# A decoder kernel's gated part: two accumulators that shared a PSUM tile get tiles of their own, one pair's last products stand two slots earlier, and the norms' mean is made on ScalarE

## The chip, the cores and the metric

The kernel runs on one core of a Trainium2 chip. The metric is the time of one execution on the device in microseconds (us). A core has five engines with a queue of instructions each, which work at the same time and wait for each other by semaphores: TensorE (PE in the profile, with PEld for its weight loads), VectorE (DVE), ScalarE (ACT), GpSimd (POOL), and SyncE (SP), which issues the transfers between the chip's memory and the core. TensorE's results go to PSUM, which the other engines read.

## The reference

Two decoder layers work on 1024 tokens of width 1024. Each has a mixer (sparse attention in the first, forgetting attention in the second) beside a cross-attention into 256 memory tokens, one output projection, and a gated feed-forward part with a causal convolution of width three. What matters here is the last:

```python
def rms_norm(x, g):
    xf = x.astype(jnp.float32)
    y = xf * lax.rsqrt(jnp.mean(xf * xf, axis=-1, keepdims=True) + EPS)
    return (y * g.astype(jnp.float32)).astype(x.dtype)
# each layer ends with
x = x + jnp.concatenate([o_mix, o_mem], axis=-1) @ w_o[l]
x = x + conv_ffn(rms_norm(x, ffn_norm[l]), w_up[l], conv_w[l], conv_b[l], w_down[l])
# and conv_ffn, with D_FF = 2816:
#   u = h @ w_up            (1024 -> 2 x 2816)
#   u = causal depthwise convolution of u over the tokens, width 3, plus conv_b
#   a, b = the two halves of u
#   return (silu(a) * b) @ w_down
```

All data are float32.

## The kernel before, in words

**Products.** Every matrix product is made as three matmuls of float32r values: each operand is split into an upper part (made by ScalarE, `upper`, L86) and the rest, the lower part (made by VectorE, `lower`, L92), and `mm3` (L166 to L168) adds upper x upper, upper x lower and lower x upper into PSUM. In the names of tiles, `wh`, `vh` and `wl`, `vl` are upper and lower parts of weights; `hx` and `hT` hold both parts of the activations. A tile can be read or written by one engine only after the engine that used it before has signalled; such a dependence is kept for the tile as a whole.

**The gated part.** The up projection (class `Up`) works on 22 pairs of weight columns (128 of each of w_up's halves). For a pair the 2 x 2 block product with the activations is made in the seven products of the Strassen-Winograd scheme, each of twelve matmuls of 128 x 512. With p, q and c for the accumulators, in order:

1. first: a11 x b11 into p, copied to c1 by ScalarE;
2. second: a12 x b21 into q; c1 + q is one quarter of the result (L2001, or L2005 in the seam);
3. third: s2 x t2 is added into p, copied to c2;
4. fourth: s1 x t1 into c, copied to c5 (L1983);
5. t3: s3 x t3 is added into p; p + c5 is a quarter (L2036, VectorE);
6. b22: s4 x b22 is added into c; c + c2 is a quarter (L2039, VectorE);
7. t4: a22 x t4 is added into p; p is the last quarter (L2042, ScalarE).

The sums s1 to s4 of weights are made by GpSimd (L1458 to L1476 in the seam, L1942 to L1950 behind it), the sums t1 to t4 of activations by VectorE and GpSimd (L1430 to L1435). Then come the convolution (L2050 on ScalarE, L2052 on VectorE), the gate (L2059) and the stores.

**PSUM.** It is used as two tiles of two banks (`psa`) and four of one bank (`psb`); a bank holds 128 x 512 float32. Before, p and c of a pair are the two halves of one `psa` tile, and q is a `psb` tile (in the seam, q is written to c's half, since c comes later).

**Order behind the seam.** `Up.run` walks over slots; pair n's product i stands at slot 7n + 2i, so that two pairs are interleaved. TensorE's order is the written one for the first 17 slots, VectorE's and ScalarE's throughout the seam; elsewhere the instruction scheduler may still move rows. Pairs 0 and 1 start in the seam and have four of their products there.

**The seam.** Between the attention and the up projection, `gated` calls `seam` (L1296 on), which finishes the output projection, adds the residual (L1379), stores x (L1385), normalises each of the eight row tiles (square and sum on ScalarE L1390, mean and eps on VectorE L1396, power on GpSimd L1394, the scaling on VectorE L1398), transposes it on TensorE (`turn`, L1611) and starts pairs 0 and 1. Its order is made by a planner (`Order`): every step has an engine, a cost, a due time, the steps it comes after and the buffers it holds (`hold`), and the planner fixes the queues of TensorE, VectorE, ScalarE and GpSimd from these.

**The norms elsewhere** (`rstd`) take a square and sum on ScalarE (L127), the mean and eps on VectorE (L128), the power on GpSimd (L130), and the scaling on VectorE (L144 and others): at the start of the kernel for the eight tiles of x and two of memory, between the layers, and at the end.

## Time and profile before

| what | us |
|---|---|
| median of three runs | 2503.85 |
| lowest and highest run | 2503.02, 2506.69 |
| the profiled execution | 2505.03 |
| its span | 2503.0 |
| TensorE busy in the span | 2428.3 |
| VectorE busy | 1884.3 |
| ScalarE busy | 1351.8 |
| GpSimd busy | 737.0 |

The profile's rows are of one execution. A row has its start from the beginning of the span and its duration in us, the engine, the line of the kernel before, the operation with output and input, and in brackets the idle time of the engine before it with what ended it. TensorE's matmuls overlap: one of 128 x 512 shows about 0.39 us, and the next starts about 0.23 after it. The mean granted clock of TensorE was 0.995 of full speed. The first layer's seam lies around 640 to 740 us, the second's 1164.2 us later.

### The profile page before, as it was taken

What the parts mean: (1) busy time and instruction counts of PE and PEld (TensorE: products, weight loads), DVE (VectorE), ACT (ScalarE), POOL (GpSimd) and SP (SyncE); (2) the same over time, 40 slices, a digit from 0 to 9 for tenths busy, and PEclk for the clock granted to TensorE, in tenths of its full rate; (3) what the DMA queues carried; (4) which work ended last, traced back from release to release, by engine and by line L of the source; (5) the groups of instructions that cost most, each with busy time, mean ns of one, the idle gap of its engine ahead of it and who ended that gap; (6) DMA issues with size and microseconds to landing.
All of it is one profiled execution on the core that took longest, in us unless ns stands there. A gap on an engine that the chain in (4) does not pass through costs nothing.

```text
span 2503.0 us, 35524 instructions
## 1 busy us (share of the span) xinstructions
PE 2428.3 (97%) x12210; PEld 2040.0 (82%) x12210; DVE 1884.3 (75%) x3182; ACT 1351.8 (54%) x2583; POOL 737.0 (29%) x620
## 2 busy tenths in 40 slices
PE   7999999998989999999999999998999999999998
PEld 7788888877868888888889988887777888888886
DVE  5657999884597787879665478878578787788765
ACT  5335988884354454454455257757254454445444
POOL 0114455454165545430000000001235545551000
PEclk9999999999999999999999999999999999999999
DMA  8465233245423333367335567666613333339433
GB/s 251 134 211 165 69 86 101 81 141 165 163 64 114 99 103 109 98 228 247 93 126 174 159 179 204 184 177 192 218 68 106 101 102 110 96 101 318 164 95 121
DMA packets 303276, 357.68 MB, mean 143 GB/s; under 512 B 38024, under 2 KB 183288, under 8 KB 303096
## 3 DMA queue, kind: packets, MB, share of 16 engines
q1 hardware_dynamic: 303096, 355.41, 45.4%
q8 instruction: 97, 1.59, 0.3%
q14 instruction: 83, 0.68, 0.1%
HBM read 245.55 MB, written 109.78 MB: 142 GB/s over the span
## 4 chain that ended last, share of the span: by engine, by line
PE 80%; DVE 8%; DMA 4%; ACT 3%; issue 2%; POOL 1%; SPq 1%; POOLq 0%; DVEq 0%; ACTq 0%
PE psa L166 12%; PE psa L167 12%; PE psa L168 12%; PE psb L166 10%; PE psb L168 9%; PE psb L167 9%; PE psa L316 5%; PE psb L448 5%; PE psb L475 5%; DVE hT L92 1%; DVE wl L92 1%; DVE pt L462 1%; ACT ps L376 1%; DMA wr<-o 1%; ACT pt L459 1%
## 5 line engine op out<-in xcount | busy, mean ns | idle before, releaser
L2052 DVE SCALAR_TENSOR_TENSOR v<-u,cw,v 128x1023 f32<-128x1023 f32 (+1 forms) x176 | 276.7, 1572 | 67.7 <-ACT v L2050 66.1
L92 DVE TENSOR_TENSOR wl<-wr,wh 128x512 fp32r<-128x512 f32 (+2 forms) x244 | 229.2, 944 | 112.6 <-ACT wh L86 112.3
L86 ACT ACTIVATE wh<-wr 128x512 fp32r<-128x512 f32 (+2 forms) x244 | 182.3, 751 | 241.6 <-PE psa L168 109.8
L462 DVE TENSOR_TENSOR pt<-psb,pt 128x512 fp32r<-128x512 f32 (+2 forms) x380 | 247.0, 659 | 60.6 <-ACT pt L459 58.2
L2050 ACT ACTIVATE v<-u,cw 128x1024 f32<-128x1024 f32 x88 | 109.6, 1246 | 306.6 <-DVE u L2039 288.6
L459 ACT ACTIVATE pt<-psb 128x512 fp32r<-128x512 f32 (+2 forms) x380 | 215.6, 575 | 95.5 <-PE psb L448 92.3
L475 PE MATMUL psb<-pt,vv 128*128 128x512 f32 (+2 forms) x864 | 220.7, 355 | 5.2 <-DVE pt L462 4.1
L166 PE MATMUL psa<-hT,wh 128*128 128x512 f32 x560 | 218.4, 390 | 3.4 <-ACT hT L86 3.3
L167 PE MATMUL psa<-hT,wh 128*128 128x512 f32 x560 | 218.1, 389 | 1.5 <-DVE hT L92 1.5
L168 PE MATMUL psa<-hT,wl 128*128 128x512 f32 x560 | 217.9, 389 | 0.0
L316 PE MATMUL psa<-kk,qq 128*128 128x512 f32 (+4 forms) x792 | 177.3, 342 | 7.0 <-ACT pm L373 3.0
L376 ACT ACTIVATE ps<-ps,stat 128x640 f32<-128x640 f32 (+4 forms) x192 | 147.7, 773 | 28.7 <-DVE stat L356 28.5
L130 POOL TENSOR_TENSOR rs<-ss,consts 128x1 f32<-128x1 f32 x24 | 13.3, 555 | 492.0 <-DVE ss L128 320.0
L166 PE MATMUL psb<-hT,wh 128*128 128x512 f32 x384 | 156.0, 406 | 0.3 <-DVE pt L462 0.3
L475 PEld LDWEIGHTS psb<-pt,vv 128*128 128x128 f32 x864 | 136.5, 190 | 21.0 <-DVE pt L462 8.2
L448 PE MATMUL psb<-consts,ps 128*128 128x128 f32 x928 | 145.9, 274 | 6.6 <-DVE pt L462 1.7
L356 DVE CUSTOM_DVE_ANT_0 ps<-psa,caub 128x128 f32<-128x128 f32 (+1 forms) x192 | 139.6, 750 | 15.2 <-PE psa L316 13.4
L168 PE MATMUL psb<-hT,wl 128*128 128x512 f32 x384 | 151.0, 393 | 0.0
L167 PE MATMUL psb<-hT,wh 128*128 128x512 f32 x384 | 150.6, 392 | 0.0
L166 PE MATMUL psa<-hx,wh 128*128 128x512 f32 x352 | 137.9, 392 | 7.0 <-DVE u L2036 5.4
L316 PEld LDWEIGHTS psa<-kk,qq 128*128 128x128 f32 x792 | 122.5, 191 | 26.3 <-DVE stat L356 6.2
L539 POOL TENSOR_TENSOR wr<-wr 128x512 f32<-128x512 f32 x16 | 22.2, 1390 | 408.1 <-DMA kd<-st 241.3
(320 smaller groups left out, 6778.5 us busy)
## 6 DMA issues: line engine op xcount, KB each, us to landing
wr<-in_w_up_dram SPq DMA_DIRECT2D x88, 512.0 KB
wr<-gd SPq DMA_DIRECT2D x154, 256.0 KB
gd<-v SPq DMA_DIRECT2D x88, 256.0 KB
o<-ob SPq DMA_DIRECT2D x128, 128.0 KB
wr<-o SPq DMA_DIRECT2D x32, 512.0 KB
hT<-in_w_down_dram SPq DMA_DIRECT2D x64, 256.0 KB
gd<-gs SPq DMA_DIRECT2D x60, 256.0 KB
qd<-st SPq DMA_DIRECT2D x56, 256.0 KB
```

The lines of the kernel that those rows point to most:

```text
L86: self.nc.scalar.activation(hi, src, AF.Copy)
L92: self.nc.vector.tensor_tensor(lo, src, f32(hi), ALU.subtract)
L166: mm(out, lh, rh, start=first, stop=False, skip_group_check=more)
L167: mm(out, lh, rl, start=False, stop=False, skip_group_check=more)
L168: mm(out, ll, rh, start=False, stop=last, skip_group_check=more)
L316: nc.tensor.matmul(out, w, rhs, start=b not in banks[:i], stop=b not in banks[i + 1:])
L376: nc.scalar.activation(p, p, AF.Exp, bias=st[:, 0, ii:ii + 1], scale=-1.0, accum_out=st[:, 1, ii:ii + 1])
L448: nc.tensor.transpose(tp[0:kb, x:x + P], br["pt"][ii][:, o:o + kb], self.ident)
L459: nc.scalar.activation(st["hi"], st["src"], AF.Copy)
L462: self.nc.vector.tensor_tensor(st["lo"], st["src"], f32(st["hi"]), ALU.subtract)
L475: self.nc.tensor.matmul(out, v, t, start=st["begin"] and i == 0, stop=st["end"] and i == len(mms) - 1)
L2052: nc.vector.scalar_tensor_tensor(v[:, d:], u[:, :S - d], cw[:, tap, i:i + 1], v[:, d:], ALU.mult, ALU.add)
```

## The change

It has three parts.

- p becomes a `psb` tile of its own, and c the first half of a `psa` tile of its own, in the seam and behind it. In the seam the planner's holds follow, the second products no longer come after the copy of p, and the third products come after that copy rather than after the sum c1 + q.
- Pair 1's products t3, b22 and t4 stand at slots 13, 15 and 17 in place of 15, 17 and 19, and the copy of its fourth product is called at slot 11 in place of 10.
- The mean with eps is made by ScalarE, an Identity activation with a bias tile `eps`, in place of VectorE's tensor_scalar, in `rstd` and in the seam.

The numbers of lines in the changed kernel are four or five higher (L2036 becomes L2040, L2039 L2043, L2042 L2046, L1983 L1988, L166 L171, L1611 L1616, L1398 L1403, L1430 L1435, L1431 L1436).

```diff
+    def mean(self, ss):
+        self.nc.scalar.activation(ss[:, 1:2], ss[:, 0:1], AF.Identity, bias=self.eps, scale=1.0 / D)
+
     def rstd(self, pool, x, junk):
         nc = self.nc
         ss = self.sb(pool, [P, 2], F32, "ss", 4)
         nc.scalar.activation(junk, x, AF.Square, accum_out=ss[:, 0:1])
-        nc.vector.tensor_scalar(ss[:, 1:2], ss[:, 0:1], 1.0 / D, EPS, ALU.mult, ALU.add)
+        self.mean(ss)
...
-            q = o.add("ACT", 1.05, square, at + 2, a, [c])
-            m = o.add("DVE", 0.2, lambda: nc.vector.tensor_scalar(s["ss", t][:, 1:2], s["ss", t][:, 0:1], 1.0 / D, EPS, ALU.mult, ALU.add), at + 2.4, [q])
-            p = o.add("POOL", 0.52, power, at + 3, [m])
+            q = o.add("ACT", 1.25, square, at + 2, a, [c])
+            p = o.add("POOL", 0.52, power, at + 3, [q])
...
-        psas = [o.hold("psa", True) for _ in range(2)]
+        psas, psbs = [o.hold("psa", True) for _ in range(2)], []
         late = []
         for n in range(2):
             def go(n=n):
-                ac = self.psa()
-                st[n]["p"], st[n]["c"] = ac[:, :CH], ac[:, CH:]
+                st[n]["p"] = self.psb()
                 up.prod(n, st[n]["p"], "a11", "b11", True)
...
         turn(7)
         for n in range(2):
             def go(n=n):
-                st[n]["q"] = st[n]["c"]
+                st[n]["q"] = st[n]["c"] = self.psa()[:, :CH]
                 up.prod(n, st[n]["q"], "a12", "b21", True)
             hs = [psas[n]] + ([ha[1]] if n == 0 else [h1])
-            x = pe(4 * MM, go, [s["w", n, "a12" if n == 0 else "ra"], s["c1", n]] + parts["b21"], hs)
-            s["early", n] = o.add("DVE", 0.6, lambda n=n: up.take_early(n), now + 1.0, [x], [psas[n]])
+            x = pe(4 * MM, go, [s["w", n, "a12" if n == 0 else "ra"]] + parts["b21"], hs)
+            s["early", n] = o.add("DVE", 0.6, lambda n=n: up.take_early(n), now + 1.0, [x, s["c1", n]], [psas[n]])
...
-            x = s["third", n] = pe(4 * MM, lambda n=n: up.prod(n, st[n]["p"], "s2", "t2", False), [s["w", n, "21"], s["early", n]] + parts["t2"], [psas[n]])
+            x = s["third", n] = pe(4 * MM, lambda n=n: up.prod(n, st[n]["p"], "s2", "t2", False), [s["w", n, "21"], s["c1", n]] + parts["t2"], [psbs[n]])
...
     def first(self, n):
         s = self.st[n]
-        ac = self.k.psa()
-        s["p"], s["c"] = ac[:, :CH], ac[:, CH:]
+        s["p"], s["c"] = self.k.psb(), self.k.psa()[:, :CH]
...
-        at(10, self.copy_fourth, 1)
+        at(11, self.copy_fourth, 1)
...
-                    i, odd = divmod(slot - 7 * n, 2)
+                    i, odd = divmod(slot - 7 * n + (2 if n == 1 else 0), 2)
```

**How the order moves.** On TensorE, from pair 0's first product on, before the change (the first row of each group of twelve; `psa_7929` is pair 0's tile, `psa_7957` pair 1's, `psa_8222` pair 2's, `psb_8255` pair 2's q; the L1611 rows are the transposes of the last row tile). The rows are, from the top: pair 0's and pair 1's first products, pair 0's second, the transposes, pair 1's second, then further on pair 0's b22 and t4, pair 2's first, pair 1's t3, pair 2's second:

```order
L166 MATMUL psa_7929<-hx_7630,vh_7592 128x512
L166 MATMUL psa_7957<-hx_7630,wh_7881 128x512
L166 MATMUL psa_7929<-hx_7639,vh_7595 128x512
L1611 MATMUL psb_7999<-consts,x_7393 128x128 x4
L1611 MATMUL psb_8004<-consts,x_7393 128x128 x4
L166 MATMUL psa_7957<-hx_7639,wh_7881 128x512
...
L166 MATMUL psa_7929<-hx_7839,wh_8035 128x512
L166 MATMUL psa_7929<-hT_8072,vh_8078 128x512
L166 MATMUL psa_8222<-hx_7630,wh_8187 128x512
L166 MATMUL psa_7957<-hT_7995,wh_8164 128x512
L166 MATMUL psb_8255<-hx_7639,wh_8187 128x512
```

And with the change, the same groups (p of pairs 0, 1, 2 is `psb_7931`, `psb_7959`, `psb_8240`, c of pairs 0 and 1 `psa_7994` and `psa_8017`):

```order
L171 MATMUL psb_7931<-hx_7633,vh_7594 128x512
L171 MATMUL psb_7959<-hx_7633,wh_7885 128x512
L1616 MATMUL psb_7980<-consts,x_7395 128x128 x4
L1616 MATMUL psb_7987<-consts,x_7395 128x128 x4
L171 MATMUL psa_7994<-hx_7643,vh_7597 128x512
L171 MATMUL psa_8017<-hx_7643,wh_7885 128x512
...
L171 MATMUL psa_7994<-hx_7844,wh_8036 128x512
L171 MATMUL psb_7931<-hT_8076,vh_8079 128x512
L171 MATMUL psb_7959<-hT_8015,wh_8166 128x512
L171 MATMUL psb_8240<-hx_7633,wh_8191 128x512
```

The transposes of the last row tile moved ahead of both second products, and pair 1's t3 ahead of pair 2's first product; b22 now writes another tile than the t3 product before it.

On ScalarE, at the end of the seam, before (`c_8113` and `c_8160` are the copies of pair 0's and pair 1's fourth products, `wh_8164` the upper part of pair 1's s3 and s4, `hT_8072` the activations t4):

```order
L1983 ACTIVATE c_8093<-psa_7957 128x512
L86 ACTIVATE hT_8072<-x_7393 128x4x128 x2
L1983 ACTIVATE c_8113<-psa_7929 128x512
L1983 ACTIVATE c_8160<-psa_7957 128x512
L86 ACTIVATE wh_8164<-ws_8116 128x1024
L2050 ACTIVATE v_8181<-u_8141,cw_7357 128x1024
```

And with the change (`wh_8166`, `c_8115` and `c_8183` are the same three):

```order
L1988 ACTIVATE c_8096<-psb_7959 128x512
L86 ACTIVATE hT_8076<-x_7395 128x4x128 x2
L86 ACTIVATE wh_8166<-ws_8120 128x1024
L1988 ACTIVATE c_8115<-psa_7994 128x512
L86 ACTIVATE hT_8076<-x_7395 128x4x128
L1988 ACTIVATE c_8183<-psa_8017 128x512
L2054 ACTIVATE v_8185<-u_8145,cw_7359 128x1024
```

The split of pair 1's s3 and s4 moved ahead of both copies.

On VectorE, around the normalisation of the last row tile, before (L1398 is that normalisation, `psb_7923` and `psb_8004` the transposes of the last tile but one and of the last):

```order
L92 TENSOR_TENSOR hx_7839<-psb_7923,hx_7839 128x4x128
L1396 TENSOR_SCALAR ss_7945<-ss_7945 128x1
L92 TENSOR_TENSOR hT_7903<-x_7393,hT_7903 128x4x128
L92 TENSOR_TENSOR wl_7906<-ws_7501,wh_7905 128x1024
L1398 SCALAR_TENSOR_TENSOR x_7393<-x_7393,rs_7955,gb_7443 128x1024
```

And with the change:

```order
L92 TENSOR_TENSOR hT_7905<-x_7395,hT_7905 128x4x128
L92 TENSOR_TENSOR wl_7909<-ws_7503,wh_7908 128x1024
L1403 SCALAR_TENSOR_TENSOR x_7395<-x_7395,rs_7953,gb_7445 128x1024
L92 TENSOR_TENSOR hx_7844<-psb_7925,hx_7844 128x4x128
L92 TENSOR_TENSOR hT_7905<-x_7395,hT_7905 128x4x128
L1435 TENSOR_TENSOR x_7395<-psb_7980,x_7395 128x512
L1436 TENSOR_TENSOR x_7395<-psb_7987,x_7395 128x512
```

The mean is gone, and the eviction of the tile before (`hx`) moved behind the normalisation.

More of the change, by code (lines that the diff above doesn't have):

```diff
@@ L105, in constants @@
         self.nhalf = c[:, C_NH:C_NH + 1]
+        self.eps = cp.tile([P, 1], F32, name="eps")
+        nc.vector.memset(self.eps, EPS)
     def masks(self, pool, keep):
@@ L1390, in square @@
                 nc.scalar.activation(self.sb(up.pool, [P, CH], F32, "c", 5).bitcast(BF16), self.x[:, t, :], AF.Square, accum_out=s["ss", t][:, 0:1])
+                self.mean(s["ss", t])
             def power():
@@ L1552, in go @@
             def go(n=n):
-                ac = self.psa()
-                st[n]["p"], st[n]["c"] = ac[:, :CH], ac[:, CH:]
+                st[n]["p"] = self.psb()
                 up.prod(n, st[n]["p"], "a11", "b11", True)
-            hs = [psas[n]] + ([ha[0]] if n == 0 else [h1])
+            psbs.append(o.hold("psb", True))
+            hs = [psbs[n]] + ([ha[0]] if n == 0 else [h1])
             x = pe(4 * MM, go, [s["w", n, "a11" if n == 0 else "ra"]] + parts["b11"], hs)
@@ L1561, in copy @@
                 st[n]["c1"] = up.copied(st[n]["p"])
-            s["c1", n] = o.add("ACT", 0.48, copy, now + 0.8, [x], [c, psas[n]])
+            s["c1", n] = o.add("ACT", 0.48, copy, now + 0.8, [x], [c, psbs[n]])
         turn(7)
@@ L1580, in copy @@
                 st[n]["c2"] = up.copied(st[n]["p"])
-            o.add("ACT", 0.48, copy, now + 1, [x], [psas[n], c])
+            o.add("ACT", 0.48, copy, now + 1, [x], [psbs[n], c])
         for n in range(2):
```

## The prediction

> **What bounds the kernel now.** I read the busy shares first, then the busy time by stretch, then what TensorE waited for in the stretches that are not full, then the single rows there. The shares, from the head of the page:
>
> ```profile
> PE 2428.3 (97%) x12210; PEld 2040.0 (82%) x12210; DVE 1884.3 (75%) x3182; ACT 1351.8 (54%) x2583; POOL 737.0 (29%) x620
> ```
>
> TensorE sets the time nearly everywhere, so only its holes are worth anything. Busy time by stretch (length, then PE, PEld, DVE, ACT, POOL, granted clock, DMA share, GB/s), first layer's seam and what follows it:
>
> ```profile
> 700.00:710.00 10.00, 7.57 (x31) 5.44 (x30) 9.90 (x11) 6.97 (x13) 9.66 (x6) 1.00 0.00 0
> 710.00:720.00 10.00, 7.44 (x33) 5.82 (x31) 10.00 (x12) 1.61 (x4) 4.44 (x4) 1.00 0.20 57
> 720.00:730.00 10.00, 8.02 (x31) 5.68 (x32) 6.67 (x6) 7.49 (x9) 6.49 (x5) 1.00 0.36 101
> 800.00:1100.00 300.00, 300.00 (x1324) 248.08 (x1323) 236.56 (x190) 144.05 (x177) 152.30 (x91) 1.00 0.33 107
> ```
>
> TensorE has holes of about 7 us in 700 to 730, and none in 800 to 1100: what is won in the seam is kept, because behind it TensorE works without a break. VectorE is full from 700 to 720. What TensorE waited for between 690 and 800 (total, times, longest); three of its six lines; the second layer gives the same six:
>
> ```profile
> PE psa L166 <- DVE u L2036: 2.7, 1, 2.7
> ...
> PE psa L166 <- DVE u L2039: 0.8, 1, 0.8
> ...
> PE psa L166 <- ACT u L2042: 0.7, 1, 0.7
> ...
> ```
>
> And the rows themselves on TensorE (start, duration; in brackets the idle time before and its releaser):
>
> ```profile
> 694.05 0.39 PE L166 MATMUL psa<-hx,vh 128*128 128x512 f32 x1
> 696.80 1.04 PE L1611 MATMUL psb<-consts,x 128*128 128x128 f32 x8
> 702.21 0.47 PE L166 MATMUL psa<-hT,wh 128*128 128x512 f32 x1 [1.63 <-ACT hT L86]
> 703.43 0.50 PE L167 MATMUL psa<-hT,wh 128*128 128x512 f32 x1 [0.75 <-DVE hT L92]
> 720.15 0.50 PE L166 MATMUL psa<-hx,wh 128*128 128x512 f32 x1 [2.71 <-DVE u L2036]
> 723.97 0.51 PE L166 MATMUL psa<-hT,vh 128*128 128x512 f32 x1 [0.79 <-DVE u L2039]
> 727.74 0.50 PE L166 MATMUL psa<-hx,wh 128*128 128x512 f32 x1 [0.73 <-ACT u L2042]
> 728.80 0.50 PE L168 MATMUL psa<-hx,wl 128*128 128x512 f32 x1 [0.32 <-DVE wl L92]
> 733.91 0.39 PE L166 MATMUL psb<-hx,wh 128*128 128x512 f32 x1
> ```
>
> In order they are: pair 0's second product; the transposes of the last tile; pair 0's third product, with a hole at its start and one at its second matmul; pair 0's b22 product, its t4 product, pair 2's first product with two holes; and at 733.91 pair 2's second product, when pair 1's t3 product is done too. The waits behind b22 are of two kinds. The t4 product really needs L2036, because it adds into p, which L2036 reads. But b22 writes c, and L2036 reads p: it waits only because p and c are halves of one tile. The same holds for t4 waiting for L2039, which reads c, and for pair 2's first product, whose new tile is pair 0's whole old one.
>
> **The change, part by part.** *The waits across the halves* are 2.71 + 0.79 + 0.73 = 4.23 us a layer. Not all of it comes back, since VectorE is late itself:
>
> ```profile
> 693.47 1.49 DVE L1398 SCALAR_TENSOR_TENSOR x<-x,rs,gb 128x1024 f32<-128x1024 f32 x1 [0.74 <-DMA xm<-x]
> 701.98 0.68 DVE L92 TENSOR_TENSOR hx<-psb,hx 128x512 fp32r<-128x512 f32 x1
> 703.30 2.31 DVE L92 TENSOR_TENSOR wl<-ws,wh 128x1024 fp32r<-128x1024 f32 x1
> 711.84 1.21 DVE L92 TENSOR_TENSOR wl<-ws,wh 128x1024 fp32r<-128x1024 f32 x1
> 719.41 0.68 DVE L2036 TENSOR_TENSOR u<-psa,c 128x512 f32<-128x512 f32 x1
> 721.64 1.22 DVE L92 TENSOR_TENSOR wl<-ws,wh 128x1024 fp32r<-128x1024 f32 x1 [1.55 <-ACT wh L86]
> 723.22 0.69 DVE L2039 TENSOR_TENSOR u<-psa,c 128x512 f32<-128x512 f32 x1 [0.36 <-PE psa L168]
> 725.34 1.85 DVE L2052 SCALAR_TENSOR_TENSOR v<-u,cw,v 128x1023 f32<-128x1023 f32 x1 [1.43 <-ACT v L2050]
> 727.12 1.62 DVE L92 TENSOR_TENSOR wl<-wr,wh 128x1024 fp32r<-128x1024 f32 x1
> ```
>
> From 693.47 to the end of L2036 at 720.09 VectorE never waits. Its list up to there keeps its work, with one more row behind the last normalisation: an hx eviction that stood ahead of it (its like at 701.98 takes 0.68, some 0.6 in a row of them, since the next starts before it has ended). So L2036 of pair 0 ends at about 720.09 + 0.6 = 720.7, and t4 cannot start before.
>
> The b22 product, in between, now waits for ScalarE's copy of c alone. In ScalarE's new order a split stands ahead of that copy, whose input is GpSimd's second sum for pair 1, and GpSimd's first sum waits for the split's lower half at 711.84:
>
> ```profile
> 713.20 1.62 POOL L1473 TENSOR_TENSOR ws<-wr,wr 128x512 f32<-128x512 f32 x1 [3.03 <-DVE wl L92]
> 714.78 1.75 POOL L1476 TENSOR_TENSOR ws<-wr,ws 128x512 f32<-128x512 f32 x1
> 719.99 0.60 ACT L1983 ACTIVATE c<-psa 128x512 f32<-128x512 f32 x1 [7.30 <-POOL u L2010]
> 720.49 1.05 ACT L86 ACTIVATE wh<-ws 128x1024 fp32r<-128x1024 f32 x1
> 724.00 1.24 ACT L2050 ACTIVATE v<-u,cw 128x1024 f32<-128x1024 f32 x1 [2.46 <-issue]
> ```
>
> With the 0.6 above, GpSimd is done at 716.53 + 0.6 = 717.1, the split (1.05) at 718.2, the copy (0.60) at 718.8, b22 (a product is twelve matmuls, 694.05 to 696.80, 2.75) at 721.6. T4 starts there and not at 723.97: **2.4 us**.
>
> *Pair 1's last products two slots sooner* put its t3 between t4 and pair 2's first product. Its lower half is what VectorE now writes at 721.64, late by 1.55 through ScalarE, where pair 1's fourth copy stands ahead of the split and waits for a buffer (719.99 and 720.49 above). The change moves that copy behind, so the lower half follows L2036 at once, 720.7 to 721.9, and t3 runs from 724.3 to 727.0. Pair 2's first product comes then, no longer waiting for L2042. Its third matmul needs the lower half of 727.12: from 720.7 on VectorE has 1.2 (wl), 0.6 (L2039), 1.24 in which it waits for the convolution's first part on ScalarE (724.00), and 1.85 for the next (L2052), then this wl of 1.62, so 720.7 + 6.5 = 727.2, in time. Both are done at 729.8 instead of 733.91: 4.1 us. I take **3.6 a layer**, between 2.4 and 4.1 and nearer the upper, which counts further down the queue; the rest I leave because pair 3's lower half is then just in time on VectorE. Without pair 1's shift, pair 2's first product would follow t4 at 724.3 and stand until 727.2: the shift covers VectorE's lag.
>
> *The last transposes ahead of both second products.* TensorE reaches them at 694.05, not 696.80, and x's tile is done at 693.47 + 1.49 = 694.96, so TensorE waits 0.9 there, and everything behind in its queue with it, the two second products first. In return the halves of the last tile are made sooner, and the holes of 1.63 and 0.75 at 702.21 and 703.43 shrink by about 1.5. But the next product that needs fresh VectorE work (pair 0's t3) comes no sooner than VectorE's list lets it. Ends: nothing, and 2.38 - 0.9 = 1.5 us a layer. I take nothing, since t4 is set by L2036 either way.
>
> *The mean on ScalarE.* 24 rows of L128 and 16 alike of L1396 go, and 40 come:
>
> ```profile
> L128 DVE TENSOR_SCALAR ss<-ss x24: 140/148/156, 6.6 to 2450.5; 128x1 f32<-128x1 f32 x24
>   POOL rs L130: 320.0, 22
> L127 ACT ACTIVATION_READ_ACCUMULATOR xn<-xl x12: 184/186/201, 6.4 to 96.9; 128x1 f32 x12
>   DMA xm<-x: 9.7, 10
> ```
>
> VectorE loses 40 x 0.148 = 5.9 us of rows, ScalarE gains 40 of about 0.19 (the nearest row of that size) = 7.5 at 54% load. Who waited for the mean is GpSimd, whose idle time costs nothing, and the last line says that the normalisation in the seam waited ten times for the store of x, not for its scale: the saving there lies ahead of a wait that stays. [...] The trace's nearest ScalarE row of one column is 0.186. [...]
>
> *The start.* Here the mean moves the order: the first normalisation comes ahead of a weight split on VectorE, the second tile's mean behind the third tile's square on ScalarE.
>
> ```profile
> 15.52 1.97 PE L159 MATMUL psb<-consts,xn 128*128 128x128 f32 x8 [3.01 <-DVE xn L144]
> 14.92 1.06 ACT L127 ACTIVATE xn<-xl 128x1024 f32<-128x1024 f32 x1 [0.34 <-DMA xl<-in_x_dram]
> 48.63 0.37 PE L166 MATMUL psb<-wh,hT 128*128 128x292 f32 x1 [2.68 <-DVE gates L1198]
> ```
>
> The third tile's load is issued some 1.7 earlier, so its square ends near 14.4; then the split (some 0.7), two means (0.4), the power (0.55) and the normalisation (1.28) put the second transposes at about 17.3, 1.8 late. The hole of 2.68 at 48.63, which hangs on a load, takes that up. Ends: 0.7 gained and 1.8 lost; I take 0.
>
> *Four more PSUM tiles of one bank at the down projection.* Its first step takes four, and the third is now pair 21's p, read last by ScalarE's copy. That copy ran at once when its product was done:
>
> ```profile
> 1121.80 0.60 ACT L2042 ACTIVATE u<-psa 128x512 f32<-128x512 f32 x1 [0.74 <-PE psa L168]
> ```
>
> Six matmuls of 0.23 (1.4 us) go to the first two tiles meanwhile, so 0.60 is covered; without that cover it costs 0.6 a layer. I take 0.
>
> **Sum.** The profiled execution took 2505.03 us (span 2503.0): 2505.03 - 2 x 3.6 = 2497.8. It lies 1.2 above the median of the runs, 2503.85, so on their footing 2496.7.
>
> **Rivals.** *VectorE gives it back.* The same split takes 2.31 at 703.30 and 1.21 at 711.84; the first lies beside GpSimd's work, which fills 9.66 of 10 us there and 4.44 of the next ten. If GpSimd's sums shift onto the fast rows, the 8.2 us from 711.84 to 720.09, of which GpSimd covers 4.4, could stretch by up to 3.8 x 0.9 = 3.4 a layer, and t4 gains 0.2 to 1.8 a layer: 2500.3 to 2503.5, say 2502. Against it: GpSimd's sums are the same, and overlap more early means less later. [...]
>
> *All holes go.* If the transposes' 1.5 holds too and L2036 comes on time (0.6), 3.6 + 1.5 + 0.6 = 5.7 a layer: 2492.5. Against it: VectorE full from 700 to 720.
>
> *The last normalisation comes late, and the kernel is slower.* TensorE and VectorE now both hang on it sooner, and its releaser is the store of x. VectorE's list behind it has no slack, so each us late is a us at t4; the gain of 3.6 is used up at 3.6 us late, and slower by 0.2% begins at 6.1. One issue of these stores took a third of 13.39 = 4.5 us on its queue:
>
> ```profile
> 675.90 13.39 SPq L1385 DMA_DIRECT2D xm<-x  x3
> ```
>
> Two of them late is 9 us, 2 x (9 - 3.6) = 11 slower: 2514.5; one is 2505.6. Against it: no load or store moves in the seam.
>
> *It doesn't do what it says*: the waits stay because some other read of the tile holds them; 2504.
>
> **How the numbers follow.** About 0.2% (5 us) can be told from no change. Forecast 0.60; VectorE gives it back 0.20; all holes go 0.10; slower 0.05; no effect 0.05. The forecast with the ends of the start and the transposes spans 2493.5 to 2499.5; the range takes in most of the two neighbours: 2491 to 2503. Faster: 0.60 x 0.95 + 0.20 x 0.2 + 0.10 = 0.71; slower 0.05; the rest, 0.24, is the same.
>
> **What would show it.** Right: at b22 no wait for L2036 but one of about 1.5 for ScalarE's copy of c, none above 0.3 at t4, pair 2's second product about 3.6 sooner against the seam's start, the same in both layers, and 800 to 1100 still full. Wrong: a wait at t4 above 1, at the first transposes above 2, or at pair 3's first product; a start later than the hole at 48.63 takes up; a hole at the down projection's first step.

## The result and the profile after

The changed kernel takes 2490.52 us (median of four runs, 2487.43 to 2494.30) against 2504.87 for the kernel before on the same chip (2503.02 to 2506.69): a ratio of 0.9943, with a 95% interval of 0.9926 to 0.9961, or 14.35 us less. Forecast were 2496.7 and a range of 2491 to 2503. The direction was right, the gain was twice the 7.2 us forecast, and the time lies 0.5 below the range. A second series gave 2489.99 (ratio 0.9948, 0.9936 to 0.9960). The profiled execution took 2489.81 us, its span is 2487.7.

Busy shares from the head of the page of the changed kernel:

```profile
PE 2424.5 (97%) x12210; PEld 2041.9 (82%) x12210; DVE 1897.2 (76%) x3143; ACT 1362.4 (55%) x2623; POOL 744.1 (30%) x620
```

TensorE does the same work. What went is idle time. Busy time by stretch, first layer's seam (length, then PE, PEld, DVE, ACT, POOL, granted clock, DMA share, GB/s):

```profile
700.00:710.00 10.00, 8.74 (x39) 6.91 (x38) 10.00 (x9) 2.36 (x5) 6.97 (x5) 1.00 0.00 0
710.00:720.00 10.00, 9.14 (x41) 7.22 (x40) 8.46 (x10) 4.85 (x6) 4.28 (x5) 1.00 0.54 159
720.00:730.00 10.00, 9.62 (x43) 7.64 (x42) 10.00 (x8) 7.09 (x8) 6.29 (x5) 1.00 0.23 68
760.00:1100.00 340.00, 340.00 (x1499) 281.24 (x1499) 274.58 (x219) 161.14 (x197) 171.27 (x104) 1.00 0.35 114
```

The holes in 700 to 730 shrink from 7.0 to 2.5 us, and 760 to 1100 is still full, so that what the seam wins is kept. The waits of TensorE between 630 and 780 (total, times, longest), all there are now:

```profile
PE psa L172 <- DVE hT L92: 1.3, 1, 1.3
PE psa L171 <- ACT c L1988: 0.9, 1, 0.9
PE psb L1616 <- DVE x L1403: 0.5, 1, 0.5
PE psb L173 <- DVE wl L92: 0.4, 1, 0.4
```

No wait for L2040, L2043 or L2046 (L2036, L2039 and L2042 before) is left. The rows on TensorE:

```profile
689.09 1.23 PE L1616 MATMUL psb<-consts,x 128*128 128x128 f32 x8 [0.45 <-DVE x L1403]
...
702.73 0.50 PE L172 MATMUL psa<-hT,wh 128*128 128x512 f32 x1 [1.26 <-DVE hT L92]
...
711.84 0.50 PE L171 MATMUL psa<-hx,wh 128*128 128x512 f32 x1 [0.86 <-ACT c L1988]
...
714.70 0.39 PE L171 MATMUL psb<-hT,vh 128*128 128x512 f32 x1
...
721.16 0.50 PE L173 MATMUL psb<-hx,wl 128*128 128x512 f32 x1 [0.38 <-DVE wl L92]
```

They are the last tile's transposes, the second matmul of pair 0's fourth product, b22, t4 (without a wait) and the third matmul of pair 2's first product.

To compare two kernels I take the start of the same matmul, by its place in TensorE's queue, at places where the order is the same in both. For the first layer's seam these are the 3915th and the 4186th matmul. Before:

```profile
690.16 0.39 PE L167 MATMUL psa<-hx,vh 128*128 128x512 f32 x1
...
760.18 0.39 PE L166 MATMUL psa<-hT,wh 128*128 128x512 f32 x1
```

After:

```profile
684.59 0.39 PE L172 MATMUL psb<-hx,vh 128*128 128x512 f32 x1
...
749.84 0.39 PE L171 MATMUL psb<-hT,wh 128*128 128x512 f32 x1
```

Before, 70.02 us lie between them, now 65.25: the seam is 4.8 us shorter. In the second layer the length is taken to a matmul 44 places further on and gives 80.01 and 75.50, 4.5 less. The start of the down projection adds 0.28 a layer, the same in every kernel below with split tiles and in no other. These make 9.9 us. The seam's first part, up to 684.59, shows 1.5 less in the first layer and 0.2 in the second. The rest of the profile's 15.3 us lies in the kernel's opening (2.2) and in the attention of both layers, where two profiles of the very same kernel differ as much (experiment 1 for the attention; at 155 us the two profiles of experiment 4 are 0.6 and 2.7 ahead of the kernel before).

In the following, "seam" is the length between these two places against the 70.02 and 80.01 of the profile before, first layer and second layer.

### The profile page after: what moved, and what is told of

It is laid out like the page before. It is cut to its first block, busy times and chain, and to the rows that moved or that the text cites. A ratio compares the mean times of both kernels' runs of the same rounds, so it can differ in the third digit from the quotient of the medians.

```text
span 2487.7 us, 35535 instructions
## 1 busy us (share of the span) xinstructions
PE 2424.5 (97%) x12210; PEld 2041.9 (82%) x12210; DVE 1897.2 (76%) x3143; ACT 1362.4 (55%) x2623; POOL 744.1 (30%) x620
## 4 chain that ended last, share of the span: by engine, by line
PE 81%; DVE 8%; ACT 3%; issue 3%; DMA 2%; POOL 1%; SPq 0%; POOLq 0%; DVEq 0%; ACTq 0%
PE psb L171 16%; PE psb L172 16%; PE psb L173 16%; PE psa L171 6%; PE psa L173 6%; PE psa L172 6%; PE psa L321 5%; PE psb L453 5%; PE psb L480 5%; DVE wl L92 1%; DVE hT L92 1%; DVE pt L467 1%; ACT ps L381 1%; ACT pt L464 1%; DVE ps L361 1%
## 5 line engine op out<-in xcount | busy, mean ns | idle before, releaser
L2056 DVE SCALAR_TENSOR_TENSOR v<-u,cw,v 128x1023 f32<-128x1023 f32 (+1 forms) x176 | 288.8, 1642 | 64.1 <-ACT v L2054 64.0
L171 PE MATMUL psb<-hT,wh 128*128 128x512 f32 x736 | 293.1, 398 | 0.4 <-DVE pt L467 0.4
L173 PE MATMUL psb<-hT,wl 128*128 128x512 f32 x736 | 287.8, 391 | 0.0
L172 PE MATMUL psb<-hT,wh 128*128 128x512 f32 x736 | 287.6, 391 | 0.0
L173 PEld LDWEIGHTS psb<-hT,wl 128*128 128x128 f32 x736 | 138.3, 188 | 29.3
L135 POOL TENSOR_TENSOR rs<-ss,consts 128x1 f32<-128x1 f32 x24 | 17.3, 720 | 482.0 <-ACT ss L127 315.9
L171 PEld LDWEIGHTS psb<-hT,wh 128*128 128x128 f32 x736 | 138.5, 188 | 27.1 <-DVE pt L467 1.1
L172 PEld LDWEIGHTS psb<-hT,wh 128*128 128x128 f32 x736 | 138.6, 188 | 25.1
L453 PEld LDWEIGHTS psb<-consts,ps 128*128 128x128 f32 x928 | 110.4, 142 | 34.0 <-DVE ps L419 4.6
```

Of the source, the lines that this page charges most:

```text
L171: mm(out, lh, rh, start=first, stop=False, skip_group_check=more)
L172: mm(out, lh, rl, start=False, stop=False, skip_group_check=more)
L173: mm(out, ll, rh, start=False, stop=last, skip_group_check=more)
L453: nc.tensor.transpose(tp[0:kb, x:x + P], br["pt"][ii][:, o:o + kb], self.ident)
L2056: nc.vector.scalar_tensor_tensor(v[:, d:], u[:, :S - d], cw[:, tap, i:i + 1], v[:, d:], ALU.mult, ALU.add)
```

## The experiments

The theory behind the forecast was: the waits across the halves of a tile are the gain, the slots cover VectorE's lag, and the mean on ScalarE is worth nothing. The rival that the result brought up was that the mean, which also moves the transposes of the last tile, pays about half.

**1. The kernel before, once more.** No edit.

> The kernel before, unchanged, for a second profile. The profile of the changed kernel lies 15.2 us ahead of the first profile of before, and some 2 us of that come in the attention of the first layer (1.45 of it between 504 and 510 us), where nothing is changed. If that is the difference of two executions, the two profiles of before differ by 1 us or more there too, in either direction, and agree within 0.2 us in the two seams. If it comes from the change, the two profiles of before agree within 0.3 us everywhere.

It took 2503.84 us. Its seams differ from those of the first profile by +0.20 and +0.03. Outside the seams the two profiles of one kernel differ more: 0.7 us in the opening and 3.9 in the first layer's attention, given back by 3.6 in the second's. So the attention's differences cannot be read as gains, and those of the seams only beyond some tenths of a us (experiment 3 has a seam that differs by 0.5 with nothing edited in it).

**2. The mean on ScalarE alone**, in the norms and the seam; tiles and slots as before. (From the kernel before; `eps` and `mean` are added as in the change. The first lines are shortened.)

```diff
-            q = o.add("ACT", 1.05, square, at + 2, a, [c])
-            m = o.add("DVE", 0.2, lambda: nc.vector.tensor_scalar(...), at + 2.4, [q])
-            p = o.add("POOL", 0.52, power, at + 3, [m])
+            q = o.add("ACT", 1.25, square, at + 2, a, [c])      # square also calls self.mean
+            p = o.add("POOL", 0.52, power, at + 3, [q])
...
-        nc.vector.tensor_scalar(ss[:, 1:2], ss[:, 0:1], 1.0 / D, EPS, ALU.mult, ALU.add)
+        self.mean(ss)
```

> Only the mean on ScalarE, both in the norms and in the seam; tiles and slots as before. This alone moves the loads of the start and, by the planner, the transposes of the last row tile ahead of both second products. Theory A (the mean's move pays by the order that follows from it): 2.2 us at the start, 1.5 where the first layer's seam begins, and 0 to 1.5 in each seam, 4 to 6 us together, with the wait of 2.7 for L2036 at b22 as long as before or longer. Theory B (all of the gain is in the split tiles and the slots; the start is one execution's luck): within 1 us of before.

2503.19 us against 2504.14, ratio 0.9997 (0.9986 to 1.0008): nothing. Its seams are 0.87 and 0.91 us longer. TensorE's holes there, transposes already ahead of both second products:

```profile
688.63 1.06 PE L1616 MATMUL psb<-consts,x 128*128 128x128 f32 x8 [0.45 <-DVE x L1403]
702.28 0.50 PE L172 MATMUL psa<-hT,wh 128*128 128x512 f32 x1 [1.19 <-DVE hT L92]
713.55 0.50 PE L171 MATMUL psa<-hx,wh 128*128 128x512 f32 x1 [3.05 <-DVE u L2041]
```

What the earlier transposes win (1.19 at pair 0's fourth product instead of 1.63 + 0.75 at its third) is waited for elsewhere: 0.45 at the transposes, 3.05 instead of 2.71 at b22, where the shared tile holds TensorE until VectorE has read p, and a little behind it. The seam's holes add up to 6.84 us in this layer, against 6.93 before. But behind the hole at b22 the granted clock drops, in both layers (to a mean of 0.81 and 0.85 in the stretches below, and of 0.72 from 1882 to 1887 in the second layer), and that lengthens the seam. Stretches of the same kernel, the first with the hole (columns as above):

```profile
711.00:716.00 5.00, 2.45 (x7) 1.93 (x8) 3.27 (x5) 1.54 (x2) 0.61 (x1) 0.81 0.89 265
716.00:721.00 5.00, 4.12 (x16) 3.04 (x15) 1.71 (x3) 2.02 (x2) 4.75 (x5) 0.85 0.16 49
```

Theory B holds for the mean by itself.

**3. The mean on ScalarE in the norms only**, the seam as before. (`eps` and `mean` are added as in the change.)

```diff
-        nc.vector.tensor_scalar(ss[:, 1:2], ss[:, 0:1], 1.0 / D, EPS, ALU.mult, ALU.add)
+        self.mean(ss)
```

> Only the mean of the norms outside the seam on ScalarE (start, between the layers, end); the seam as before. Theory A: about 2.2 us from the start alone, all of it there by 60 us, and both seams' waits as before within 0.2 us. Theory B: within 1 us of before.

2502.41 against 2504.14, ratio 0.9992 (0.9983 to 1.0002). Nothing that can be told from no change; the middle, 1.7, lies between the theories, and the interval holds both. The seams, where nothing is edited, are 0.46 and 0.24 us shorter, with a wait of 1.4 instead of 2.7 at b22 in the first layer, behind a stretch at half clock (mean granted clock 0.77 from 700 to 705), and without the 0.32 at pair 2's first product in both: more than the 0.2 expected, so a seam's length differs by up to 0.5 between executions. The first transposes come 2.4 us sooner and the second 1.8 later, as in the changed kernel, and the hole of 2.68 at 48.63 is gone in exchange. It is gone in all seven profiles with this opening; the seven with the old one have it, with 0.24 to 2.68 us. At 155 us the former are 0.5 to 2.5 ahead of the profile before, the latter, without that profile itself, 0.5 to 2.7. So the opening is worth nothing that shows.

**4. Tiles and slots, the mean left on VectorE.**

```diff
-        self.mean(ss)
+        nc.vector.tensor_scalar(ss[:, 1:2], ss[:, 0:1], 1.0 / D, EPS, ALU.mult, ALU.add)
...  and the same in the seam, as a step of its own on VectorE
```

> The split tiles and pair 1's last products two slots sooner, the mean on VectorE as before. The transposes of the last row tile stay behind pair 0's second product. The prediction's terms: 3.6 us a layer, between 2.4 and 4.1, nothing at the start: 7 us together. Theory A: the same 7 to 8.5. Theory B: nearly all of the 14, that is 12 or more. In both the wait of 2.7 for L2036 is gone.

2492.60 against 2504.14, ratio 0.9951 (0.9936 to 0.9966): 8.5 to 16 us, with the middle, 11.5, between the two theories. Seams 3.51 and 3.60 shorter, which is the 3.6 a layer forecast for these two parts. A second series of the same kernel, with the changed kernel beside it on one chip:

> The kernel with the tiles and slots changed and the mean left on VectorE, a second time, on the chip of the changed kernel: what the mean on ScalarE is worth on top. Theory A (its new orders pay at the start and at the transposes): 3 to 4 us behind the changed kernel (1.5 at the start, 1 a layer). Theory B (it is worth nothing, as alone): within 1.

2493.64 against 2489.99 for the changed kernel and 2502.37 for the one before (ratio 0.9966, 0.9953 to 0.9979); seams 3.15 and 3.35 shorter. Over both series tiles and slots give 3.4 a layer, and 3.65 us are missing to the changed kernel. The two ratios' intervals overlap, but the seams do not (3.15 to 3.60 here, 4.46 to 4.77 for the change): the mean does pay on top of tiles and slots, as Theory A had it, though not at the opening, which was 2.7 ahead here too, with the mean on VectorE.

**5. Tiles alone**, slots and mean as before.

```diff
-                    i, odd = divmod(slot - 7 * n + (2 if n == 1 else 0), 2)
+                    i, odd = divmod(slot - 7 * n, 2)
...
-        at(11, self.copy_fourth, 1)
+        at(10, self.copy_fourth, 1)
```

(from the kernel of experiment 4)

> The split tiles alone: pair 1's products in their old slots, the mean on VectorE. By the prediction the slots cover VectorE's lag: without them pair 2's first product follows pair 0's t4 and stands at its third matmul until VectorE has the lower half, to about 727.2 on the clock of the first layer before. So the gain is 1 to 2.5 us a layer smaller than with the slots, 3 to 5 us in all. If the slots bring nothing, it is as with the slots, 7 us or more.

2497.23 against 2503.62, ratio 0.9975 (0.9964 to 0.9986); seams 1.84 and 2.08 shorter. The waits across the halves are gone, and a new one stands at pair 2's first product (`psb<-hx,wh` here), which now follows t4 behind two matmuls of pair 1's b22 (`psa<-hx,wh`) that the instruction scheduler moved up:

```profile
722.05 0.80 PE L171 MATMUL psb<-hx,wh 128*128 128x512 f32 x1 [2.15 <-ACT wh L86]
722.65 0.63 PE L172 MATMUL psb<-hx,wh 128*128 128x512 f32 x1
...
723.50 0.63 PE L171 MATMUL psa<-hx,wh 128*128 128x512 f32 x1
723.93 0.63 PE L172 MATMUL psa<-hx,wh 128*128 128x512 f32 x1
```

The prediction put this hole at 2.9 us (724.3 to 727.2) and laid it to VectorE's lower half. It is 2.15, and what is late is ScalarE's upper half. The rows behind the hole take 0.63 instead of 0.39 and start 0.43 apart instead of 0.23: half clock again (mean 0.70 from 720 to 725). In the second layer the same hole has no such stretch behind it (1.00 from 1880 to 1900).

**6. The slots alone**, shared tiles and mean as before.

```diff
-                    i, odd = divmod(slot - 7 * n, 2)
+                    i, odd = divmod(slot - 7 * n + (2 if n == 1 else 0), 2)
...
-        at(10, self.copy_fourth, 1)
+        at(11, self.copy_fourth, 1)
```

> Pair 1's last products two slots sooner alone: p and c as halves of one tile, the mean on VectorE. b22 and t4 of pair 0 wait as before (2.7 and 0.8), pair 2's first product no longer waits for the copy of p (0.7), since t3 of pair 1 stands between: 0.3 to 1.2 us a layer, under 2.5 in all. If most of the gain is in the slots, 5 us or more.

2511.47 against 2503.62, ratio 1.0027 (1.0016 to 1.0037): slower, which no theory expected. Seams 3.88 and 3.16 longer. TensorE's holes from pair 0's t3 product on:

```profile
718.68 0.50 PE L166 MATMUL psa<-hT,wh 128*128 128x512 f32 x1 [2.42 <-ACT c L1983]
722.55 0.50 PE L166 MATMUL psa<-hx,wh 128*128 128x512 f32 x1 [0.84 <-DVE u L2036]
726.35 0.51 PE L166 MATMUL psa<-hT,vh 128*128 128x512 f32 x1 [0.78 <-DVE u L2039]
736.66 0.50 PE L166 MATMUL psa<-hx,wh 128*128 128x512 f32 x1 [1.80 <-DVE u L2036]
```

And ScalarE beside the first of them:

```profile
717.08 1.06 ACT L86 ACTIVATE wh<-ws 128x1024 fp32r<-128x1024 f32 x1 [4.54 <-POOL ws L1476]
718.05 0.58 ACT L1983 ACTIVATE c<-psa 128x512 f32<-128x512 f32 x1
```

With the slots, the split of pair 1's s3 and s4 stands ahead of the copy of pair 0's c on ScalarE. In the changed kernel only b22 waits for that copy. With shared tiles the t3 product waits too, one product sooner, since it writes p beside c. And pair 1, moved forward, now has its own wait across the halves, 1.80 at 736.66, with a stretch at half clock behind it (the matmuls from 737.74 on show 0.63). The slots are only worth something with split tiles: they give 1.4 a layer there (3.4 against 1.96), and cost 3.5 without.

**7. The changed kernel with the old slots.**

```diff
-                    i, odd = divmod(slot - 7 * n + (2 if n == 1 else 0), 2)
+                    i, odd = divmod(slot - 7 * n, 2)
...
-        at(11, self.copy_fourth, 1)
+        at(10, self.copy_fourth, 1)
```

> The changed kernel with pair 1's last products back in their old slots. By the same reasoning 1 to 2.5 us a layer are lost against the changed kernel: 9 to 12 us ahead of before in place of 14. If the slots bring nothing: 14.

2495.77 against 2503.62, ratio 0.9970 (0.9953 to 0.9986); seams 2.31 and 1.83 shorter. The hole of 2.2 at pair 2's first product is there as in experiment 5, with half clock behind it in both layers (mean 0.80 from 725 to 730, 0.74 from 1885 to 1890). So the slots are worth 2.3 and 2.7 a layer in the changed kernel, and the mean gives nothing while that hole stands (2.07 with it, 1.96 without).

**8. The changed kernel, once more.** No edit.

> The changed kernel once more, nothing edited, on one chip with the next three. Its first times lay 14.35 us under the kernel before (9.8 to 18.5), while the holes that went in its profile add up to about 12: 4.8 and 4.5 in the two gated parts, 0.6 at the down projection, some 1.5 to 2 at the start. Theory A (the holes are the whole of it): 11 to 13 ahead of the kernel before. Theory B (something that one profile does not show goes too, such as stretches at half the TensorE clock behind long holes): 14 or more.

2489.99 against 2502.37, ratio 0.9948 (0.9936 to 0.9960), or 10 to 16 us; seams 4.46 and 4.60 shorter. Its seams have no stretch at half clock, as in the first profile (granted clock 1.00 there from 640 to 760 and from 1780 to 1900; in this one a mean of 0.998 over the whole run). The interval does not tell Theory A from B.

**9. The last transposes back between the second products.**

```diff
-        turn(7)
         for n in range(2):
+            if n == 1:
+                turn(7)
```

> The changed kernel with the last tile's transposes put back between the two second products; mean on ScalarE, tiles and slots stay as changed. Theory A (the earlier transposes pay 1 us a layer once the waits across the halves are gone, since they shorten the hole ahead of pair 0's third product from 2.4 to 1.3): seam 3.5 shorter than before the change instead of 4.8 and 4.5, so 2 to 2.5 us behind the changed kernel, and the hole of 2.4 is back, in some of its places followed by a stretch at half clock. Theory B (the prediction's: VectorE's list sets t4 either way, the transposes are worth nothing): within 0.5 of the changed kernel.

2499.86 against 2502.37, ratio 0.9988 (0.9979 to 0.9996): some 10 us behind the changed kernel, far more than either theory said. Seams 0.38 and 0.21 shorter. It is not the clean test that I meant: the planner also wrote four halves of hT for other products ahead of the transposes' evictions on VectorE. VectorE's rows, with the last normalisation first, and then TensorE's holes:

```profile
688.40 1.94 DVE L1403 SCALAR_TENSOR_TENSOR x<-x,rs,gb 128x1024 f32<-128x1024 f32 x1 [1.58 <-DMA xm<-x]
690.26 0.68 DVE L92 TENSOR_TENSOR hx<-psb,hx 128x512 fp32r<-128x512 f32 x1
690.86 5.18 DVE L92 TENSOR_TENSOR hT<-x,hT 128x512 fp32r<-128x512 f32 x4
695.97 0.68 DVE L1435 TENSOR_TENSOR x<-psb,x 128x512 f32<-128x512 f32 x1
```

```profile
698.65 0.50 PE L171 MATMUL psb<-hT,wh 128*128 128x512 f32 x1 [3.52 <-ACT hT L86]
701.60 0.80 PE L172 MATMUL psb<-hT,wh 128*128 128x512 f32 x1 [2.46 <-DVE hT L92]
```

The holes at pair 0's third product become 6.0 us together, again with half clock behind it (the matmuls from 702.20 to 706.04 show 0.63). What it shows is that the order around the last tile can cost 4 us a layer, not what the transposes' place is worth by itself.

**10. That place by itself**: every mean on VectorE, the planner's order as in the changed kernel. (From the changed kernel.)

```diff
-        self.mean(ss)
+        nc.vector.tensor_scalar(ss[:, 1:2], ss[:, 0:1], 1.0 / D, EPS, ALU.mult, ALU.add)
...
-                self.mean(s["ss", t])
 
             def power():
+                nc.vector.tensor_scalar(s["ss", t][:, 1:2], s["ss", t][:, 0:1], 1.0 / D, EPS, ALU.mult, ALU.add)
                 s["rs", t] = self.sb(pool, [P, 1], F32, "rs", 4)
```

> Tiles and slots changed, every mean left on VectorE, but the last tile's transposes ahead of both second products as in the changed kernel (the mean is written with the power, so that the planner sets the order without it). What the mean on ScalarE gives on top of tiles and slots, 1.0 to 1.3 a layer in the gated part, is either the order or the rows. Theory A (the order: the hole ahead of pair 0's third product shrinks from 2.4 to 1.3): seam 4.5 to 4.8 shorter than before the change, 2491, and no stretch at half clock there. Theory B (the rows taken from VectorE): seam 3.2 to 3.6 shorter, 2493 to 2494.

2494.11 against 2503.08, ratio 0.9962 (0.9948 to 0.9976); seams 3.98 and 3.47 shorter: nearer to Theory B. The hole shrinks as Theory A had it, to 1.26 (at pair 0's fourth product now), and no half clock follows (no matmul of 128 x 512 from 684 to 728 shows over 0.50). But the transposes now wait longer, since the last normalisation comes later. VectorE's row, then TensorE's:

```profile
687.34 1.72 DVE L1403 SCALAR_TENSOR_TENSOR x<-x,rs,gb 128x1024 f32<-128x1024 f32 x1 [1.03 <-DMA xm<-x]
```

```profile
689.21 1.23 PE L1616 MATMUL psb<-consts,x 128*128 128x128 f32 x8 [1.02 <-DVE x L1403]
```

In the changed kernel the same two are

```profile
686.62 2.32 DVE L1403 SCALAR_TENSOR_TENSOR x<-x,rs,gb 128x1024 f32<-128x1024 f32 x1
```

and the 0.45 at 689.09 above. The starts mislead, since a row that starts later here takes less time; what counts for the transposes and for VectorE's list is where it ends. Laid on the clock of the profile before by the seam's first place (5.57 and 6.02 later), the normalisation ends at 694.96 before, at 695.08 here and at 694.51 in the changed kernel. In the second layer, where the store of x ends none of these waits, it ends at 1859.11, 1859.25 and 1858.66, the same distances within 0.02. So with the mean on ScalarE the last normalisation is done 0.45 us sooner than before the change, and 0.6 sooner than here.

What it waits for here, in the second layer, is its scale. Its row, then the mean on ScalarE and the same normalisation in the changed kernel:

```profile
1850.15 2.31 DVE L1403 SCALAR_TENSOR_TENSOR x<-x,rs,gb 128x1024 f32<-128x1024 f32 x1 [0.44 <-POOL rs L1400]
```

```profile
1844.15 0.30 ACT L127 ACTIVATE ss<-ss,eps 128x1 f32<-128x1 f32 x1
1845.93 2.32 DVE L1403 SCALAR_TENSOR_TENSOR x<-x,rs,gb 128x1024 f32<-128x1024 f32 x1
```

The mean on VectorE comes 0.66 us later than ScalarE's (counted from the seam's first place), behind other rows of a full queue, and the power that needs it ends 1.2 later. Those 0.6 us run through to the end: here VectorE's fourth lower half, ScalarE's copy of c, b22 and t4 all come 0.55 to 0.61 later than in the changed kernel, in both layers. At t4 the four layers of the two profiles of the change agree within 0.04 us, so these small parts can be told apart there: counted from the seam's first place, t4 starts at 30.1 in the changed kernel, at 30.7 here and at 30.9 to 31.2 in experiment 4 (33.8 before). So up to t4 the mean's move is worth 0.6 a layer and the order 0.2 to 0.5, the upper value where half clock follows the hole ahead of pair 0's third product. A better place for the mean on VectorE was not tried.

**11. A try at the rest**: ScalarE's copy of c ahead of the split of pair 1's s3 and s4, and pair 0's convolution one slot later.

```diff
-                    at(7 * n + slot, f, n)
+                    at(7 * n + slot + (1 if n == 1 and f == self.split_34 else 0), f, n)
...
-                at(7 * n + slot, self.conv, n, h, tap)
+                at(7 * n + slot + (1 if n == 0 else 0), self.conv, n, h, tap)
```

> The changed kernel with pair 1's second split one slot later, so that ScalarE's copy of c stands ahead of it, and pair 0's convolution one slot later, so that VectorE's lower halves for pair 1 and pair 2 stand ahead of it. Theory A (ScalarE's order and the convolution are what is left): no wait of 0.86 at b22, t4 0.7 sooner, no wait of 0.38 in pair 2's first product, 1.0 a layer, 2 in all. Theory B (VectorE's list is full and the holes only move on): within 0.5.

2491.27 against 2502.37, ratio 0.9956 (0.9942 to 0.9970), the changed kernel's own within the intervals; seams 4.43 and 4.42 shorter, no better. The waits at b22 and in pair 2's first product are gone and t4 comes 0.6 sooner, with a wait of 0.42 for L2040 now; but one of their size stands at pair 3's first product, whose lower half VectorE makes at 741.18, behind the convolution's rows that were put off. TensorE's row, then VectorE's:

```profile
743.57 0.50 PE L173 MATMUL psb<-hx,wl 128*128 128x512 f32 x1 [1.54 <-DVE wl L92]
```

```profile
738.34 1.73 DVE L92 TENSOR_TENSOR wl<-ws,wh 128x1024 fp32r<-128x1024 f32 x1
739.99 1.27 DVE L2056 SCALAR_TENSOR_TENSOR v<-u,cw,v 128x1023 f32<-128x1023 f32 x1
741.18 2.33 DVE L92 TENSOR_TENSOR wl<-wr,wh 128x1024 fp32r<-128x1024 f32 x1
```

Theory B. No kernel of these beats the changed one.

The seams side by side, in us against the kernel before (first, second layer; of kernels with two profiles both):

| kernel | seam | ratio of the times |
|---|---|---|
| before, again | +0.2, +0.0 | |
| mean alone | +0.9, +0.9 | 0.9997 |
| mean in the norms only | -0.5, -0.2 | 0.9992 |
| slots alone | +3.9, +3.2 | 1.0027 |
| tiles alone | -1.8, -2.1 | 0.9975 |
| tiles and mean | -2.3, -1.8 | 0.9970 |
| tiles and slots | -3.5, -3.6; -3.2, -3.4 | 0.9951; 0.9966 |
| tiles, slots, transposes' place | -4.0, -3.5 | 0.9962 |
| all (the change) | -4.8, -4.5; -4.5, -4.6 | 0.9943; 0.9948 |

## Why the prediction was right or wrong

**The waits across the halves, and the slots: right in kind, the size by choice.** No wait for L2036, L2039 or L2042 is left, b22 waits for the copy of c, nothing stands at t4, both layers gain alike, and 760 to 1100 is full. The term was 3.6 a layer; tiles and slots without the mean measured 3.51, 3.60, 3.15 and 3.35. That this is so near is in part luck: 3.6 was picked between 2.4 and 4.1, and both of these were worked out with VectorE 0.6 late, from an eviction that the kernel of experiment 4 does not move. That the slots cover a lag that would else stand at pair 2's first product is shown by experiments 5 and 7, though the lag is ScalarE's and not VectorE's. That the slots alone would make it slower was not foreseen.

**The mean on ScalarE at nothing: this step failed.** The prediction said that the normalisation in the seam waits for the store of x and not for its scale, so that "the saving there lies ahead of a wait that stays". It read one line of that view and not the next, which has a wait of 2.1 for the scale (at the first row tile):

```profile
  DMA xm<-x: 9.7, 10
  POOL rs L1394: 2.1, 1
```

And for the last row tile, on which the products hang, the store costs nothing before the change: with a wait of 0.74 for it (first layer) and with none (second) the row ends 4.80 us behind the seam's first place. Nor is it tied to the mean's engine: it is there in the first layer of experiment 9, with the mean on ScalarE (1.58), and missing in the second series of experiment 4, with the mean on VectorE. What sets that row is VectorE's full queue, in which the mean and the `hx` eviction stand ahead of it, or, with the eviction put behind it and the mean still on VectorE, the scale (experiment 10). By itself the mean's move is indeed worth nothing (experiment 2). With tiles and slots it is worth 4.59 - 3.40 = 1.2 a layer (means of the four values each), together with the order that the planner makes of it. Experiment 10 divides the part up to t4: 0.6 from the mean's engine, 0.2 to 0.5 from the order. The rest lies behind t4, in the wait in pair 2's first product, which differs between executions (0.4 to 0.7 in the change, 0.3 to 1.0 in experiments 4 and 10).

**"T4 is set by L2036 either way", with L2036 0.6 later: wrong, by the same cause.** On the clock of the profile before (5.57 added), VectorE's fourth lower half, the copy and L2040 stand in these rows of the changed kernel:

```profile
705.51 1.21 DVE L92 TENSOR_TENSOR wl<-ws,wh 128x1024 fp32r<-128x1024 f32 x1
```

```profile
711.21 0.58 ACT L1988 ACTIVATE c<-psa 128x512 f32<-128x512 f32 x1
```

```profile
713.28 0.69 DVE L2040 TENSOR_TENSOR u<-psb,c 128x512 f32<-128x512 f32 x1
```

L2040 ends at 719.54, and not at the 720.7 of the prediction (720.09 before). The lower half starts at 711.08, 0.76 sooner than before and not 0.6 later: the normalisation ends 0.45 sooner, and although the `hx` eviction does stand behind it now (0.6), the rows between take 0.3 less, because in the new order the nine halves of hT among them take 10.6 us instead of 11.5 (one takes 0.68 to 1.80). Rows that read PSUM, which in these profiles only VectorE and ScalarE have, take 0.68 or 0.69 there in either order. GpSimd's sums, the split and the copy follow it, so that the copy ends at 717.36 and not at 718.8, b22 starts at 717.41, with a wait of 0.86 instead of some 1.5, and t4 at 720.27 instead of the predicted 721.6 (723.97 before). It is the copy, not L2036, that sets t4. Pair 1's t3 and pair 2's first product are done at 723.56 (the start of the next product), on that clock 729.13, against 729.8 predicted and 733.91 before. That is 4.78 sooner; the prediction worked out 4.1 and took 3.6.

**The transposes:** predicted was a wait of 0.9 and no gain. Measured are 0.45, and a gain of the order that they belong to of 0.2 to 0.5 a layer at t4.

**The start: right.** The second transposes come at 17.24, for 17.3 predicted, and the hole at 48.63 took that up.

**The down projection:** predicted 0, with 0.6 as the cost if uncovered. It gains 0.28 a layer. Before, three matmuls at 1111 to 1119 start 0.04 to 0.11 us late, together 0.2, and after the change none does; no run shows why.

**The rivals.** VectorE gave nothing back. The case that all holes go, 5.7 a layer, named the two things that happened (transposes, and L2036 on time), at 4.6 and not 5.7. That its 2492.5 is the nearest to the measured time is in part luck, since some of that time is in no row. The slower case did not come: the store of x came late in experiments 9 and 10 (1.58 and 1.03), as before the change (0.74), and neither was slower than the kernel before.

**The sum.** 2 x 4.59 + 2 x 0.28 = 9.7 us are shown in rows, and another 0.24 at the transposes of the norm between the layers, which every profile with that mean on ScalarE has and no other: 9.9, or 2.7 more than the 7.2 forecast. The times say 9.8 to 18.5 and 10 to 16. So the rows explain 2.7 of the 7.2 us by which the gain was missed, and with them alone the time would have lain inside the range. What the rest is stays open: the seam's first part shows 1.5 and 1.2 less in the first layer in the two profiles of the change, 0.25 in the second profile of the kernel before, and 0.6 to 1.3 less in the others (0.4 more with the slots alone); the opening and the attention differ too much between executions to be read.

## What to carry to other kernels

When an accumulator shares a tile with another, the wait across the halves can hide how much the steps ahead are worth. A saving that measures nothing alone (the mean) can pay once that wait is gone, and a reorder that pays afterwards (the slots) can cost before; so such parts are tried together and apart. And a moved row is costed by what is late behind it: here the last normalisation, done 0.45 us sooner, came through VectorE, GpSimd and ScalarE to the product that sets the end. A wait in brackets is judged by where the row behind it ends, and in each layer: the wait for the store looked binding in one layer and was not there in the other.

## What the runs showed of the hardware

**A hole of 2 us can cost more than its length.** In the gated parts of the 14 profiles there are 27 holes of TensorE of 2.1 us or more (taking as one those that lie within 2 us of each other, and the two of experiment 9). Behind 16 of them six to eight matmuls of 128 x 512 show 0.63 us instead of 0.39 and start 0.43 apart instead of 0.23, which costs 1.0 to 1.6 us (eleven and twelve in experiment 9, 2.4 and 2.6), as in the rows of experiment 5. Of some 50 holes of 0.6 to 1.7 none was followed by such a stretch, and one of 1.80 was. The same hole in the same kernel had one in one layer and none in the other (experiment 5: 2.15 in the first, with; 2.16 in the second, without).

The granted clock (the last column but two) shows where these stretches lie. Each such stretch is 3.41 us at half clock (6.83 in experiment 9), and within one profile all of them begin a whole number of 3.41 us apart. Counted from them in steps of 3.41, experiment 5 has these two, the first with the hole of 2.15:

```profile
718.56:721.97 3.41, 1.34 (x6) 0.75 (x4) 1.98 (x3) 2.16 (x2) 2.35 (x2) 1.00 0.39 117
721.97:725.38 3.41, 3.33 (x8) 2.61 (x9) 3.41 (x3) 3.14 (x5) 3.41 (x3) 0.50 0.02 5
```

In the kernel before, the longer hole of 2.71 at b22 falls into two steps, 1.21 and 1.50 idle, and the clock stays at 1.00:

```profile
715.24:718.65 3.41, 2.20 (x10) 1.50 (x8) 3.41 (x5) 0.00 (x0) 1.29 (x1) 1.00 0.24 65
718.65:722.06 3.41, 1.91 (x8) 1.60 (x9) 1.86 (x4) 1.54 (x2) 0.94 (x1) 1.00 0.90 258
```

In the gated parts all 17 stretches follow a step in which TensorE is idle for 1.80 to 2.92 us; of the other steps at full clock only one reaches 1.80 (1.84, experiment 5, second layer), the next has 1.72. So in these profiles it is the idle time within one such step, not the length of the hole, that goes with the drop; no run shows why. What follows at once may hide the cost: in experiment 1 the stretch fell ahead of b22 (mean granted clock 0.73 from 700 to 705), and the wait there was 1.4 instead of 2.7. The changed kernel has no hole above 1.26 in its seams, and no such stretch there in either profile.

**A one-column activation on ScalarE is not as cheap as its accumulator read.** The group of the 40 means:

```profile
L127 ACT ACTIVATE ss<-ss,eps 128x1 f32<-128x1 f32 x40 | 11.5, 291 | 1.0
```

It takes 0.291 us each, 11.5 in all, where the prediction took 0.19 from the accumulator read (0.186 before the change) and 7.5. It cost TensorE nothing that a row shows.
